# Layer 1's decode rows: sums over partitions in plain float32, four rows at a time in the four column groups

## The chip, the core and the metric

The kernel runs on one core of one Trainium2 chip. Its engines work side by side, each on its own queue of instructions: TensorE (PE, with its weight loads PEld), VectorE (DVE), ScalarE (ACT), GpSimd (POOL), and SyncE (SP), which here only issues DMAs. The metric is the time of one execution in microseconds on the device, as the median of several runs.

## What is computed

One inference step of two layers, a retention layer and a sliding-window attention layer, for a prompt of 1024 tokens and for eight sample rows of one token each. The change touches the sample rows of the first layer: each row and head has a state S of 256 x 512, which is updated and read with the row's q.

```python
def step(S, inp):
    qc, kc, vc = inp
    inner = jnp.einsum('bthd,bshd->bhts', qc, kc) * dmask[None]
    o = jnp.einsum('bhts,bshe->bthe', inner, vc) \
        + jnp.einsum('bthd,bhde->bthe', qc, S) * cross_decay[None, :, :, None]
    S_new = S * chunk_decay[None, :, None, None] \
        + jnp.einsum('bshd,bshe->bhde', kc * k_decay[None, :, :, None], vc)
    return S_new, o
```

With one token a row this is S_new = g S + k v and o = q S_new, a sum over 256 elements of the head's key dimension. Then o is normed over its 512 values and goes on to the gate and the output projection; S_new is an output.

## The kernel before

**The stage.** The input projection of layer 1 is the first big stage. It is cut into sets of weight columns (q, k and v of each of four heads, then the gates), and each set is computed in seven block products (SEQ7) for each half of the prompt's tokens. All float32 products are made from two fp32r parts, hi and lo, as three matmuls: `product` does this at L333 to L335 for v and at L340 to L342 for the others, into PSUM tiles that the page calls b. `w_hi` (L219, ScalarE) and `w_lo` (L224, VectorE or GpSimd) make the two parts of the weights, `w_sum` (L200 to L209, GpSimd) the sums that the block products need, and `evac` (L369 to L381) takes the results out of PSUM.

**The decode rows.** Beside that stage run the 64 decode rows: four heads (h), two halves of the state's 512 columns (hf), eight rows (b). For one of them `dec_load` fetches the state (st, 128 partitions x 2 x 256) and the row's v; `dec_kv` (L263, ScalarE) and `dec_st` (L266, VectorE) update the state; `dec_y0` (L270, ScalarE) and `dec_y1` (L274, VectorE) multiply it by q and add its two halves, so that yd (128 x 256) is left, to be summed over the 128 partitions. That sum is TensorE's: `dec_yh` (L278, ScalarE) and `dec_yl` (L282, GpSimd) split yd into hi and lo, and `dec_mm` (L288, L289) multiplies both by `oneh_r[:, b, :]`, a stationary 128 x 8 of which column b is ones. So row b of the PSUM tile od (8 x 256 for each hf) collects the sum. There is one buffer for yl, two for yh and yd.

**Behind a head's 16 rows.** `dec_n1` to `dec_n4` norm od (8 x 512), `dec_tr` makes four transposes of it (L103, through `tr`), and `dec_ev` copies the result to odT, which a later stage reads.

**What sets the order.** All engines run in the order in which the code is written, which a small planner makes: the block products fill slots one after the other on a planned clock (`slot`, `prod_slot`), and all other work gets a planned time (`when`). Row by row the planner adds STEP = 5.3 us to t0; a row's steps stand at t0 plus 10.5 (kv), 12.3 (st), 13.9 (y0), 15.3 (y1), 16.8 (yh), 18.2 (yl) and 20.4 (the two matmuls), and the end of a head at offsets from its last matmuls (m). Matmuls are held in a list of their own (pes) and are put ahead of the first slot that starts after their time. The planned times set only the order; the engines run as semaphores let them.

**The one-hot.** It comes as 64 columns of the constant c1, is loaded at L645 and cast to fp32r at L653 on VectorE.

Of the kernel before, what the change touches and what calls it, by code (L numbers as in the profile page):

```python
# [7 lines left out]
F32 = mybir.dt.float32  # L8
F32R = mybir.dt.float32r
AF = mybir.ActivationFunctionType  # L10
# [6 lines left out]
ND = 8  # L17
# [17 lines left out]
def make_consts():  # L35
    p = np.arange(128, dtype=np.float64)
    ident = np.eye(128)
    mask = np.zeros((128, H, 128))
    kdec = np.zeros((128, H, NCH))
    epsg = np.zeros((128, H))  # L40
    for h in range(H):
        g = GAM[h]
        mask[:, h, :] = np.where(p[None, :] >= p[:, None], g ** (-(p[:, None] + 1.0)) / 16.0, 0.0)
        for c in range(NCH):
            kdec[:, h, c] = g ** (SREF - 128.0 * c - p - 1.0) / 16.0
        epsg[:, h] = EPS * g ** (-2.0 * (p + 1.0))
    onehot = np.zeros((128, 8, 8))
    for b in range(8):
        onehot[:, b, b] = 1.0
    c1 = np.concatenate([a.reshape(128, -1) for a in (ident, mask, kdec, epsg, onehot)], 1)  # L50
# [12 lines left out]

def trunk(tc, x_prompt, x_sample, state_ret, cache_k, cache_v, norm_ret, w_in_ret, ret_out_norm,
          w_out_ret, norm_swa, w_in_swa, q_norm, k_norm, sinks, w_out_swa, c1, c2,
          y_p, y_s, nrp, nrs, nkp, nvp, nks, nvs):
    nc = tc.nc
    ctx = ExitStack()
    with ctx:
        ctx.enter_context(tc.manual_schedule(engines=MS))  # L70
        _trunk(ctx, tc, nc, locals())


def _trunk(ctx, tc, nc, a):
# [20 lines left out]
    mm = nc.tensor.matmul  # L95
# [6 lines left out]
    def tr(out, in_, ident, start=True, stop=True):  # L102
        nc.tensor.matmul(out, in_, ident, is_transpose=True, start=start, stop=stop)  # L103


    ident = cp.tile([128, 128], F32, name="ident")
# [25 lines left out]
    dcp = sa.enter_context(tc.tile_pool(name="dcp", bufs=1, reuse_waits="tile"))  # L132
# [11 lines left out]
    oneh_r = dcp.tile([128, 8, 8], F32R, name="oneh_r")  # L144
    warm = dcp.tile([1, 8], F32, name="warm")

    XT = {}
# [95 lines left out]
    heads = [dict() for _ in range(H)]  # L243
# [4 lines left out]
    def dt(name, bufs, sh=(128, 256), dt_=F32):  # L248
        return dpo[0].tile(list(sh), dt_, name=name, bufs=bufs)

    def sview(x, h, hf, b):
        return x[0, b, h, :, hf * 256:hf * 256 + 256].rearrange("(f p) e -> p f e", p=128)
# [13 lines left out]
        dve.scalar_tensor_tensor(d["st"], d["st"], GAM[h], d["kv"], MUL, ADD)  # L266

    def dec_y0(d, h, hf, b):
        d["yd"] = dt("yd", 2)
        act(d["yd"], d["st"][:, 0, :], AF.Copy, scale=heads[h]["qd"][:, 0, b:b + 1])  # L270
        nc.sync.dma_start(out=sview(nrs, h, hf, b), in_=d["st"])

    def dec_y1(d, h, hf, b):
        dve.scalar_tensor_tensor(d["yd"], d["st"][:, 1, :], heads[h]["qd"][:, 1, b:b + 1], d["yd"], MUL, ADD)  # L274

    def dec_yh(d, h, hf, b):
        d["yh"] = dt("yh", 2, dt_=F32R)
        act(d["yh"], d["yd"], AF.Copy)  # L278

    def dec_yl(d, h, hf, b):  # L280
        d["yl"] = dt("yl", 1, dt_=F32R)
        pool.tensor_tensor(d["yl"], d["yd"], d["yh"].bitcast(F32), SUB)  # L282

    def dec_mm(d, h, hf, b):
        if hf == 0 and b == 0:
            heads[h]["od"] = odp.tile([128, 512], F32, name="od")
        od = heads[h]["od"][0:8, hf * 256:hf * 256 + 256]
        mm(od, oneh_r[:, b, :], d["yh"], start=(b == 0), stop=False)  # L288
        mm(od, oneh_r[:, b, :], d["yl"], start=False, stop=(b == ND - 1))  # L289

    def dec_n1(h):
        d = heads[h]
        d["on"] = ring("c")[0:8, 0:512]
        d["ss"] = dcp.tile([128, 1], F32, name="oss", bufs=2)
        act(d["on"], d["od"][0:8, :], AF.Square, accum_out=d["ss"][:8])

    def dec_n2(h):
        ss = heads[h]["ss"][:8]
        dve.tensor_scalar(ss, ss, 1.0 / DV, EPS, MUL, ADD)

    def dec_n3(h):
        ss = heads[h]["ss"][:8]
        rsq(ss, ss, 1)

    def dec_n4(h):
        d = heads[h]
        dve.tensor_scalar(d["on"], d["od"][0:8, :], d["ss"][:8], None, MUL)

    def dec_tr(h):
        pt = heads[h]["pt"] = odp.tile([128, 512], F32, name="od")  # L310
        for i in range(4):
            tr(pt[:, i * 8:i * 8 + 8], heads[h]["on"][:, i * 128:i * 128 + 128], ident[:8, :8])

    def dec_ev(h):
        dve.tensor_copy(odT[:, 4 * h:4 * h + 4, :], heads[h]["pt"][:, :32].rearrange("p (i t) -> p i t", i=4))


    SEQ7 = (("A11", B11, 0, True), ("S2", T2, 1, True), ("S1", T1, 2, True), ("A12", B21, 0, False),
# [90 lines left out]

    gb = sp.tile([128, D], F32, name="gb")  # L410
    gl = sp.tile([25, 128], F32, name="gl")
    onehot = sp.tile([128, 64], F32, name="onehot")
# [128 lines left out]
    def later(n, fn, *a):  # L541

        at.setdefault(n, []).append((fn, a))

    def when(t, fn, *a):
        ev.append((t, len(ev), fn, a))
# [106 lines left out]
    later(14, lambda: dve.tensor_copy(oneh_r, onehot.rearrange("p (b m) -> p b m", b=8)))  # L653

    later(17, lambda: [fn(T3, c) for c in (5, 7) for fn in (th, tl)])
    later(18, dsums, 1, (T3,))
# [7 lines left out]
    for s in sets[2:]:  # L664
# [31 lines left out]
        for r in range(2 * s.subs):  # L696
            free = raws[-5] + 1.6
            need = min(reads[r])
            t = max(free, need - 13.0)
            t = raw_t[0] = max(t, raw_t[0] + 0.01)  # L700
# [18 lines left out]
            s.end = clock[0]  # L719

    STEP, GAP = 5.3, 6.5
    pes = []
# [85 lines left out]
    for n, s in enumerate(slots):  # L808
        while pes and pes[0][0] <= s.t:
            _, fn, args = pes.pop(0)  # L810
# [7 lines left out]
        while ev and ev[0][0] < end:  # L818
            _, _, fn, args = ev.pop(0)
# [33 lines left out]
    kdec = M01[:, 256:288].rearrange("p (h c) -> p h c", h=H)  # L853
    epsg = M01[:, 288:292]
# [886 lines left out]
    out = so_all()  # L1741
# [49 lines left out]
    pt = dec_cache(0)  # L1791
# [5 lines left out]
    pt = dec_cache(1)  # L1797
# [53 lines left out]


def c1w():
    return 128 + 512 + 32 + 4 + 64


def c2w():
# [31 lines left out]
```

## Time and profile before

| | us |
|---|---|
| median of 3 runs | 1369.84 |
| lowest, highest | 1367.8, 1372.5 |
| the profiled execution, its own time | 1371.73 |
| its span, from the first to the last instruction | 1369.9 |
| TensorE busy, its mean granted clock | 1318.6, 0.987 |

How the profile is read: each row of a timeline has the start and the length in us, the engine, the line of the kernel, the operation, out<-in by the kernel's names, the shapes, and how many instructions are merged in it. Matmuls are pipelined and their ends are modelled, so two that follow each other overlap in it; what one costs is the distance from its start to the next one's. A row that names stretches has the busy time of each engine in each, then the granted TensorE clock, the DMA engines' share and GB/s. The chain of waits follows back from the last instruction, step by step, what released it.

### The profile page before, as it was taken

Reading aid. Unit: us, or ns where it says so; the run is one execution under the profiler, and the core shown is the slowest. Engines: PE = TensorE matmul, PEld = TensorE weight load, DVE = VectorE, ACT = ScalarE, POOL = GpSimd, SP = SyncE. Lnnn points to the kernel's source line nnn. Section 1 sums busy time; section 2 is a strip of 40 time slices with the busy share of each in tenths; the row PEclk is TensorE's granted clock in tenths of the full one; section 3 lists DMA queues with packets and bytes.
Section 4 is the critical chain, followed back from the end, with each engine's and each line's share of the span. In section 5 each row is a group of like instructions: output and inputs, shape, how many; then the busy total and the mean of one; then the engine's idle time right before and its main releaser. Section 6 shows DMA issues by size and latency. Waiting matters only on the chain.

```text
span 1369.9 us, 26110 instructions
## 1 busy us (share of the span) xinstructions
PE 1318.6 (96%) x9661; PEld 1235.3 (90%) x9661; DVE 708.4 (52%) x1362; ACT 651.4 (48%) x1625; POOL 762.7 (56%) x886
## 2 busy tenths in 40 slices
PE   6999999999999999898979999998999999999998
PEld 6999999999999999686868889997898999998998
DVE  6943665566556553675751112335555555669421
ACT  5532555555556653675740112244465666657311
POOL 6753656655566753697986553544476666555000
PEclk9999999999999999999989999999999999999999
DMA  6314767667667653556545444442111110103523
GB/s 218 103 56 144 219 212 230 174 217 230 198 216 212 216 155 93 185 175 194 169 149 168 123 154 124 133 132 66 47 48 61 44 41 32 55 17 110 164 83 83
DMA packets 192804, 186.68 MB, mean 136 GB/s; under 512 B 12724, under 2 KB 172524, under 8 KB 192660
## 3 DMA queue, kind: packets, MB, share of 16 engines
q1 hardware_dynamic: 155840, 148.87, 35.8%
q10 hardware_dynamic: 36836, 36.14, 8.2%
q8 instruction: 76, 1.25, 0.4%
q14 instruction: 52, 0.43, 0.1%
HBM read 128.59 MB, written 57.41 MB: 136 GB/s over the span
## 4 chain that ended last, share of the span: by engine, by line
PE 87%; DVE 4%; POOL 3%; DMA 2%; issue 2%; ACT 1%; SPq 0%; ACTq 0%; POOLq 0%; DVEq 0%
PE b L340 7%; PE b L342 7%; PE b L341 7%; PE pj L1090 6%; PE pj L1091 6%; PE pj L1092 6%; PE pj L1141 4%; PE pj L1139 4%; PE pj L1140 4%; PE b L334 4%; PE b L333 4%; PE b L335 4%; PE tr L103 4%; PE o L1554 2%; PE tr L862 1%
## 5 line engine op out<-in xcount | busy, mean ns | idle before, releaser
L340 PE MATMUL b<-xh,woh 128*128 128x258 f32 x784 | 222.2, 283 | 0.0
L342 PE MATMUL b<-xh,wol 128*128 128x258 f32 x784 | 221.7, 283 | 0.0
L341 PE MATMUL b<-xl,woh 128*128 128x258 f32 x784 | 221.4, 282 | 0.0
L1090 PE MATMUL pj<-A_hi,wh 128*128 128x384 f32 (+1 forms) x512 | 178.6, 349 | 0.0
L1091 PE MATMUL pj<-A_lo,wh 128*128 128x384 f32 (+1 forms) x512 | 165.2, 323 | 0.0
L1092 PE MATMUL pj<-A_hi,wl 128*128 128x384 f32 (+1 forms) x512 | 165.1, 323 | 0.0
L340 PEld LDWEIGHTS b<-xh,woh 128*128 128x128 f32 x784 | 148.1, 189 | 1.2
L341 PEld LDWEIGHTS b<-xl,woh 128*128 128x128 f32 x784 | 148.7, 190 | 0.0
L342 PEld LDWEIGHTS b<-xh,wol 128*128 128x128 f32 x784 | 148.1, 189 | 0.0
L1080 POOL TENSOR_TENSOR wl<-wr,wh 128x1024 fp32r<-128x1024 f32 (+1 forms) x60 | 115.1, 1929 | 43.4 <-DVE wh L1079 20.1
L334 PE MATMUL b<-wol,xh 128*128 128x256 f32 x448 | 126.0, 281 | 1.2 <-DVE wol L224 1.2
L333 PE MATMUL b<-woh,xh 128*128 128x256 f32 x448 | 125.8, 281 | 0.0
L335 PE MATMUL b<-woh,xl 128*128 128x256 f32 x448 | 125.7, 281 | 0.0
L1090 PEld LDWEIGHTS pj<-A_hi,wh 128*128 128x128 f32 x512 | 97.3, 190 | 10.3 <-issue 9.6
L282 POOL TENSOR_TENSOR yl<-yd,yh 128x256 fp32r<-128x256 f32 x64 | 56.4, 881 | 80.9 <-PE od L289 39.0
L1091 PEld LDWEIGHTS pj<-A_lo,wh 128*128 128x128 f32 x512 | 97.5, 190 | 0.0
L1092 PEld LDWEIGHTS pj<-A_hi,wl 128*128 128x128 f32 x512 | 97.1, 190 | 0.0
L1531 POOL TENSOR_TENSOR s<-s,sm 128x512 f32<-128x512 f32 x64 | 68.0, 1062 | 50.2 <-DVE sm L1530 48.3
L224 POOL TENSOR_TENSOR wol<-raw,woh 128x512 fp32r<-128x512 f32 x52 | 68.9, 1332 | 48.1 <-ACT woh L219 47.3
L334 PEld LDWEIGHTS b<-wol,xh 128*128 128x128 f32 x448 | 84.3, 188 | 1.4 <-DVE wol L224 1.4
L333 PEld LDWEIGHTS b<-woh,xh 128*128 128x128 f32 x448 | 84.3, 188 | 0.7
L335 PEld LDWEIGHTS b<-woh,xl 128*128 128x128 f32 x448 | 84.4, 188 | 0.0
(360 smaller groups left out, 3704.9 us busy)
## 6 DMA issues: line engine op xcount, KB each, us to landing
raw<-in_w_in_ret_dram ACTq DMA_DIRECT2D x44, 512.0 KB
st<-in_state_ret_dram SPq DMA_DIRECT2D x64, 256.0 KB
out_dram<-st SPq DMA_DIRECT2D x64, 256.0 KB
wr<-in_w_out_ret_dram SPq DMA_DIRECT2D x32, 512.0 KB
wr<-in_w_in_swa_dram SPq DMA_DIRECT2D x18, 512.0 KB
vb<-vscr SPq DMA_DIRECT2D x64, 128.0 KB
evp<-qks SPq DMA_DIRECT2D x32, 256.0 KB
evx<-vsc SPq DMA_DIRECT2D x32, 256.0 KB
```

What stands on the lines that cost most here:

```text
L224: eng.tensor_tensor(lo, src_of(s, name, sub), hi.bitcast(F32), SUB)
L333: mm(dst, xh, wh, start=a and i == 0, stop=False, skip_group_check=True)
L334: mm(dst, xh, wl, start=False, stop=False, skip_group_check=True)
L335: mm(dst, xl, wh, start=False, stop=z, skip_group_check=True)
L340: mm(dst, wh, xh, start=a, stop=False, **sg)
L341: mm(dst, wh, xl, start=False, stop=False, **sg)
L342: mm(dst, wl, xh, start=False, stop=z, **sg)
L1080: lo_eng[0].tensor_tensor(lo[:, js, :], raw[:, i:i + step, :], hi.bitcast(F32)[:, js, :], ALU.subtract)
L1090: mm(ps, hi[:, k, fs], xh[:, k, t0:t1], start=first and k == ks[0], stop=False)
L1091: mm(ps, hi[:, k, fs], xl[:, k, t0:t1], start=False, stop=False)
L1092: mm(ps, lo[:, k, fs], xh[:, k, t0:t1], start=False, stop=last and k == ks[-1])
L1531: nc.gpsimd.tensor_tensor(st[:, :, 0:256], st[:, :, 0:256], sm.unsqueeze(2).broadcast_to([128, 2, 256]), ALU.mult)
```

## The change

The split into yh and yl goes, and with it `dec_yh`, `dec_yl` and their two steps in the plan. The matmuls of four rows (b = 4r to 4r + 3) are issued together, 18.0 us behind the fourth row's t0, and in plain float32: row g of the four goes to partitions 32 g to 32 g + 31 of od, with a stationary of 128 x 32 (`oneh[:, r, :]`) of which column r is ones. So a group of rows is four matmuls, each in its own 32 columns of the array; r is 0 or 1, and of the 128 partitions of od eight hold a row (0, 1, 32, 33, ...) and the others zeros. The norm then works on 128 partitions, the transposes are 128 x 128, and `dec_ev` picks out the eight. The one-hot is filled by GpSimd at the start in place of the load and the cast; yd has five buffers.

```diff
     def dec_y0(d, h, hf, b):
-        d["yd"] = dt("yd", 2)
+        d["yd"] = dt("yd", 5)
...
-    def dec_yh(d, h, hf, b):
-        d["yh"] = dt("yh", 2, dt_=F32R)
-        act(d["yh"], d["yd"], AF.Copy)
-
-    def dec_yl(d, h, hf, b):
-        d["yl"] = dt("yl", 1, dt_=F32R)
-        pool.tensor_tensor(d["yl"], d["yd"], d["yh"].bitcast(F32), SUB)
-
-    def dec_mm(d, h, hf, b):
-        if hf == 0 and b == 0:
+    def dec_mm(ds, h, hf, r):
+        if hf == 0 and r == 0:
             heads[h]["od"] = odp.tile([128, 512], F32, name="od")
-        od = heads[h]["od"][0:8, hf * 256:hf * 256 + 256]
-        mm(od, oneh_r[:, b, :], d["yh"], start=(b == 0), stop=False)
-        mm(od, oneh_r[:, b, :], d["yl"], start=False, stop=(b == ND - 1))
+        for g, d in enumerate(ds):
+            mm(heads[h]["od"][32 * g:32 * g + 32, hf * 256:hf * 256 + 256], oneh[:, r, :], d["yd"], start=(r == 0 and hf == 0),
+               stop=(r == 1), skip_group_check=(hf == 1))
...
-            tr(pt[:, i * 8:i * 8 + 8], heads[h]["on"][:, i * 128:i * 128 + 128], ident[:8, :8])
+            tr(pt[:, i * 128:i * 128 + 128], heads[h]["on"][:, i * 128:i * 128 + 128], ident)
...
-        dve.tensor_copy(odT[:, 4 * h:4 * h + 4, :], heads[h]["pt"][:, :32].rearrange("p (i t) -> p i t", i=4))
+        dve.tensor_copy(odT[:, 4 * h:4 * h + 4, :].rearrange("p i (r g) -> p i g r", g=4),
+                        heads[h]["pt"].rearrange("p (i g x) -> p i g x", i=4, g=4)[:, :, :, 0:2])
...
-        nc.scalar.dma_start(out=onehot, in_=a["c1"][:, c1w() - 64:])
...
-    later(14, lambda: dve.tensor_copy(oneh_r, onehot.rearrange("p (b m) -> p b m", b=8)))
...
-                for dt_, fn in ((0.0, dec_load), (10.5, dec_kv), (12.3, dec_st), (13.9, dec_y0), (15.3, dec_y1),
-                                (16.8, dec_yh), (18.2, dec_yl)):
+                for dt_, fn in ((0.0, dec_load), (10.5, dec_kv), (12.3, dec_st), (13.9, dec_y0), (15.3, dec_y1)):
                     when(t0 + dt_, fn, d, h, hf, b)
-                pes.append((t0 + 20.4, dec_mm, (d, h, hf, b)))
-                m = t0 + 20.4
+                ds.append(d)
+                if b % 4 == 3:
+                    pes.append((t0 + 18.0, dec_mm, (ds, h, hf, b // 4)))
+                    ds = []
+                m = t0 + 18.0
...
     dve.memset(warm, 0.0)
+    pool.memset(oneh, 0.0)
+    for r in range(2):
+        pool.memset(oneh[:, r, r:r + 1], 1.0)
```

In dec_n1 to dec_n4 the slices [0:8] and [:8] are gone; that is all that changes there.

TensorE at the fourth row of head 0, before (od is the rows' PSUM tile, b_2138 the next block product's; lines 333 to 335 are the three matmuls of a product):

```order
L354 MATMUL vd<-wol,xdecr 40x256
L288 MATMUL od<-yh,oneh_r 8x256
L289 MATMUL od<-yl,oneh_r 8x256
L333 MATMUL b_2138<-woh,xh 128x256
L334 MATMUL b_2138<-wol,xh 128x256
L335 MATMUL b_2138<-woh,xl 128x256
```

And after, where the product's lines are 323 to 325:

```order
L323 MATMUL b_2021<-woh,xh 128x256
L324 MATMUL b_2021<-wol,xh 128x256
L325 MATMUL b_2021<-woh,xl 128x256
L277 MATMUL od<-yd,oneh 32x256 x4
L323 MATMUL b_2060<-woh,xh 128x256
L324 MATMUL b_2060<-wol,xh 128x256
L325 MATMUL b_2060<-woh,xl 128x256
```

The pair of each row is gone from its place, and the four of a group stand together between two products, a little ahead of where the fourth row's pair stood.

GpSimd in the same part of the program, before (s are sums of weights, wol their lo parts, kd the decayed k of the rows):

```order
L407 TENSOR_SCALAR kd<-evp 128x2
L282 TENSOR_TENSOR yl<-yd,yh 128x256 x2
L224 TENSOR_TENSOR wol<-raw,woh 128x512 x2
L206 TENSOR_TENSOR s_2295<-raw 128x512
L206 TENSOR_TENSOR s_2300<-raw 128x512
L282 TENSOR_TENSOR yl<-yd,yh 128x256
L209 TENSOR_TENSOR s_1966<-raw,s_1966 128x512
L282 TENSOR_TENSOR yl<-yd,yh 128x256
```

And after:

```order
L397 TENSOR_SCALAR kd<-evp 128x2 x2
L221 TENSOR_TENSOR wol<-raw,woh 128x512 x2
L203 TENSOR_TENSOR s_2263<-raw 128x512
L203 TENSOR_TENSOR s_2266<-raw 128x512
L206 TENSOR_TENSOR s_1953<-raw,s_1953 128x512
```

The weights' operations follow each other as before, without the yl between them.

VectorE ahead of the first block products, before (xl are lo parts of the activations):

```order
L498 TENSOR_TENSOR xl<-rT,xh 128x4x2
L653 CAST oneh_r<-onehot 128x64
L224 TENSOR_TENSOR wol<-raw,woh 128x512 x2
L224 TENSOR_TENSOR wol<-s_904,woh 128x512
L224 TENSOR_TENSOR wol<-s_946,woh 128x512
```

And after:

```order
L487 TENSOR_TENSOR xl<-rT,xh 128x4x2
L221 TENSOR_TENSOR wol<-raw,woh 128x512 x2
L221 TENSOR_TENSOR wol<-s_904,woh 128x512
L221 TENSOR_TENSOR wol<-s_946,woh 128x512
L476 TENSOR_TENSOR xl<-u,xh 128x4x128 x2
```

The cast is gone from ahead of the lo parts; nothing else moved there.

More of the change, by code (lines that the diff above doesn't have):

```diff
@@ L46, in make_consts @@
         epsg[:, h] = EPS * g ** (-2.0 * (p + 1.0))
[L47 to L50, printed above, removed]
+    c1 = np.concatenate([a.reshape(128, -1) for a in (ident, mask, kdec, epsg)], 1)
     u = np.arange(256, dtype=np.float64)
@@ L143, in _trunk @@
     xdecd = dcp.tile([128, 4, 40], F32R, name="xdecd")
-    oneh_r = dcp.tile([128, 8, 8], F32R, name="oneh_r")
+    oneh = dcp.tile([128, 2, 32], F32, name="oneh")
     warm = dcp.tile([1, 8], F32, name="warm")
@@ L274, in dec_y1 @@
         dve.scalar_tensor_tensor(d["yd"], d["st"][:, 1, :], heads[h]["qd"][:, 1, b:b + 1], d["yd"], MUL, ADD)
-    def dec_yh(d, h, hf, b):
-        d["yh"] = dt("yh", 2, dt_=F32R)
-        act(d["yh"], d["yd"], AF.Copy)
-    def dec_yl(d, h, hf, b):
-        d["yl"] = dt("yl", 1, dt_=F32R)
-        pool.tensor_tensor(d["yl"], d["yd"], d["yh"].bitcast(F32), SUB)
-    def dec_mm(d, h, hf, b):
-        if hf == 0 and b == 0:
+    def dec_mm(ds, h, hf, r):
+        if hf == 0 and r == 0:
             heads[h]["od"] = odp.tile([128, 512], F32, name="od")
-        od = heads[h]["od"][0:8, hf * 256:hf * 256 + 256]
-        mm(od, oneh_r[:, b, :], d["yh"], start=(b == 0), stop=False)
-        mm(od, oneh_r[:, b, :], d["yl"], start=False, stop=(b == ND - 1))
+        for g, d in enumerate(ds):
+            mm(heads[h]["od"][32 * g:32 * g + 32, hf * 256:hf * 256 + 256], oneh[:, r, :], d["yd"], start=(r == 0 and hf == 0),
+               stop=(r == 1), skip_group_check=(hf == 1))
     def dec_n1(h):
         d = heads[h]
-        d["on"] = ring("c")[0:8, 0:512]
+        d["on"] = ring("c")[:, 0:512]
         d["ss"] = dcp.tile([128, 1], F32, name="oss", bufs=2)
-        act(d["on"], d["od"][0:8, :], AF.Square, accum_out=d["ss"][:8])
+        act(d["on"], d["od"], AF.Square, accum_out=d["ss"])
     def dec_n2(h):
-        ss = heads[h]["ss"][:8]
+        ss = heads[h]["ss"]
         dve.tensor_scalar(ss, ss, 1.0 / DV, EPS, MUL, ADD)
     def dec_n3(h):
-        ss = heads[h]["ss"][:8]
+        ss = heads[h]["ss"]
         rsq(ss, ss, 1)
@@ L306, in dec_n4 @@
         d = heads[h]
-        dve.tensor_scalar(d["on"], d["od"][0:8, :], d["ss"][:8], None, MUL)
+        dve.tensor_scalar(d["on"], d["od"], d["ss"], None, MUL)
     def dec_tr(h):
@@ L411, in _trunk @@
     gl = sp.tile([25, 128], F32, name="gl")
-    onehot = sp.tile([128, 64], F32, name="onehot")
     rdec = sp.tile([128, 8, ND], F32, name="rdec")
@@ L721, in _trunk @@
     STEP, GAP = 5.3, 6.5
-    pes = []
+    pes, ds = [], []
     t0 = 0.0
@@ L1853, in c1w @@
 def c1w():
-    return 128 + 512 + 32 + 4 + 64
+    return 128 + 512 + 32 + 4
 def c2w():
```

## The prediction

> **What bounds the kernel now.** I read the busy table of the page first, then the busy time by stretches, then the chain of waits inside the stretch that the change touches.
>
> ```profile
> PE 1318.6 (96%) x9661; PEld 1235.3 (90%) x9661; DVE 708.4 (52%) x1362; ACT 651.4 (48%) x1625; POOL 762.7 (56%) x886
> ```
>
> TensorE is busy 96% of the span and no other engine over 56%. The decode rows' matmuls lie between 135 and 512 us, so I asked for that stretch alone, and for the chain that ends last in it.
>
> ```profile
> core 0: us, PE busy (x) PEld busy (x) DVE busy (x) ACT busy (x) POOL busy (x), PEclk, DMA share, GB/s
> 135.00:512.00 377.00, 377.00 (x3158) 372.37 (x3157) 224.12 (x373) 210.01 (x481) 230.19 (x264) 1.00 0.68 208
> by line: PE b L340 20.5%; PE b L342 20.3%; PE b L341 20.3%; PE b L334 10.6%; PE b L333 10.6%; PE b L335 10.5%; PE od L289 2.0%; PE od L288 2.0%; PE vd L353 1.5%; PE vd L354 1.5%; PE od L103 0.4%
> ```
>
> The first row says that TensorE has work in all 377 us, at full clock. The second is stricter: every share of the chain belongs to a PE line, and together they make 100% up to rounding. No wait for VectorE, ScalarE, GpSimd or a DMA ends last anywhere here. So in this stage a microsecond of TensorE's own work is a microsecond of the run, and a microsecond taken from ScalarE or GpSimd is worth nothing. The lines to watch are L288, L289 and L103 of od: 2.0 + 2.0 + 0.4% of 377 us, some 16.6 us.
>
> **The change, part by part.** First what goes from TensorE: two fp32r matmuls for each of 64 rows.
>
> ```profile
> 146.10 0.28 PE L342 MATMUL b<-xh,wol 128*128 128x258 f32 x1
> 146.22 0.28 PE L288 MATMUL od<-yh,oneh_r 128*8 128x256 f32 x1
> 146.33 0.28 PE L289 MATMUL od<-yl,oneh_r 128*8 128x256 f32 x1
> 146.45 0.28 PE L340 MATMUL b<-xh,woh 128*128 128x258 f32 x1
> ```
>
> The durations overlap, so a matmul's price is the distance between starts: 146.10 to 146.45 is three matmuls in 0.35 us, 0.117 each. Removed: 128 x 0.117 = **15.0 us** (the chain's 4.0% of 377 us is 15.1).
>
> What comes: 16 groups of four plain float32 matmuls of 256 columns, each in its own 32 columns of the array. The trace has none with four groups, but it has plain float32 in two column groups, L1554 in the second layer (stationary 64 wide, output in partitions 0 to 63 and 64 to 127). A plain float32 call leaves two matmul records: L862 makes 64 such calls in the program and has 128 records.
>
> ```profile
> L862 PE MATMUL tr<-evp x128: 275/275/553, 547.1 to 697.3; 128*128 128x128 f32 x128
> 983.46 0.34 PE L1090 MATMUL pj<-A_hi,wh 128*128 128x384 f32 x1
> 983.64 0.33 PE L1091 MATMUL pj<-A_lo,wh 128*128 128x384 f32 x1
> 983.81 0.33 PE L1092 MATMUL pj<-A_hi,wl 128*128 128x384 f32 x1
> 984.07 0.44 PE L1554 MATMUL o<-ptf,vv 128*64 128x128 f32 x4
> 984.44 0.44 PE L1090 MATMUL pj<-A_hi,wh 128*128 128x384 f32 x1
> 984.72 0.34 PE L1091 MATMUL pj<-A_lo,wh 128*128 128x384 f32 x1
> ...
> 988.44 0.34 PE L1092 MATMUL pj<-A_hi,wl 128*128 128x384 f32 x1
> 988.71 0.66 PE L1554 MATMUL o<-ptf,vv 128*64 128x128 f32 x8
> 989.29 0.44 PE L1090 MATMUL pj<-A_hi,wh 128*128 128x384 f32 x1
> 989.57 0.34 PE L1091 MATMUL pj<-A_lo,wh 128*128 128x384 f32 x1
> ```
>
> A 384-column neighbour costs 0.175 us (983.46 to 983.81 is two). From the start of the neighbour before to the second start behind is 0.91 us for two calls (x4) and 1.13 for four (x8); less two neighbours, 0.56 and 0.78. So two further calls, one in each column group, cost 0.22: two steps of 0.11, each carrying both groups. What is left, 0.56 - 0.22 = **0.34 us, is fixed**: the price of going into the column groups and out again.
>
> For the new group I take the fixed 0.34 and two steps that carry all four column groups. A step at 256 columns is 2 x 0.11 = 0.22. So 0.34 + 0.44 = 0.78 us a group, 16 x 0.78 = **12.5 us**; TensorE gains 2.5. The unknown is the number of steps a group, since four column groups at once are not in the trace: two if all go together as L1554's two do, four if only pairs do, eight if none (16 x 2.10 = 33.6 us). I take two, the row that is nearest. For the fixed part the other end is nothing, as for L288, whose eight columns cost only 0.117; but L288 is fp32r and never leaves partition 0, and L1554 shares with the new form both type and placing, so I take 0.34.
>
> The four transposes of a head now read 128 rows, not 8.
>
> ```profile
> 233.81 0.28 PE L342 MATMUL b<-xh,wol 128*128 128x258 f32 x1
> 234.03 0.41 PE L103 MATMUL od<-ident,evc 8*128 8x8 f32 x4
> 234.37 0.39 PE L340 MATMUL b<-xh,woh 128*128 128x258 f32 x1
> 234.59 0.29 PE L341 MATMUL b<-xl,woh 128*128 128x258 f32 x1
> 1003.76 0.35 PE L1092 MATMUL pj<-A_hi,wl 128*128 128x384 f32 x1
> 1003.94 0.60 PE L103 MATMUL tr<-ident,s 128*128 128x128 f32 x4
> 1004.30 0.42 PE L1090 MATMUL pj<-A_hi,wh 128*128 128x384 f32 x1
> 1004.55 0.33 PE L1091 MATMUL pj<-A_lo,wh 128*128 128x384 f32 x1
> ```
>
> By the same reckoning the small ones cost 0.78 - 2 x 0.12 = 0.54 us and full ones 0.79 - 2 x 0.175 = 0.44: a transpose 16 times as large is cheaper, because it does not leave the full array. Four heads: **-0.4 us**.
>
> The cast of the one-hot goes, and it stood on VectorE right before an operand that TensorE waited for.
>
> ```profile
> 70.45 0.18 DVE L653 CAST oneh_r<-onehot 128x64 fp32r<-128x64 f32 x1
> 70.55 2.37 DVE L224 TENSOR_TENSOR wol<-raw,woh 128x512 fp32r<-128x512 f32 x2
> 72.37 0.39 PE L334 MATMUL b<-wol,xh 128*128 128x256 f32 x1 [1.19 <-DVE wol L224]
> ```
>
> TensorE idles 1.19 us until that product; the cast pushes it back 0.10 (70.45 to 70.55), at most its 0.18. I take **-0.1 us**.
>
> What costs or brings nothing:
>
> ```profile
> L282 POOL TENSOR_TENSOR yl<-yd,yh 128x256 fp32r<-128x256 f32 x64 | 56.4, 881 | 80.9 <-PE od L289 39.0 <-ACT yh L278 28.0 <-ACT yd L270 6.6
> L278 ACT ACTIVATE yh<-yd 128x256 fp32r<-128x256 f32 x64 | 26.3, 411 | 36.9 <-DVE yd L274 34.6 <-PE od L289 1.3 <-PE b L342 0.9
> 403.66 1.18 DVE L274 SCALAR_TENSOR_TENSOR yd<-st,qd,yd 128x256 f32<-128x256 f32 x1 [2.31 <-ACT yd L270]
> 407.22 0.28 PE L340 MATMUL b<-xh,woh 128*128 128x258 f32 x1
> 4.30 0.18 POOL L437 TENSOR_SCALAR ss<-ss 8x1 f32<-8x1 f32 x1 [3.05 <-ACT junk L433]
> ```
>
> - yh and yl: 26.3 us of ScalarE, 56.4 of GpSimd and 80.9 us of GpSimd's waits go, most of these for TensorE itself. They lie beside a TensorE that never waits, so the gain is 0.
> - The new wait: a group is issued when the last of its four yd is due. The tightest of the 16 is the last group of head 2: the order puts it just ahead of the product whose first matmul starts at 407.22 before the change, and its last yd ends at 403.66 + 1.18 = 404.84. That leaves 2.4 us, and no other group has less. Were it late, all products queued behind it on TensorE would wait, microsecond for microsecond.
> - Five yd buffers: a buffer comes round after five rows, when its group has been issued at least one row's step (5.3 us by the planner) earlier.
> - The norm over 128 partitions in place of 8, and the copy of the same 32 values: off TensorE, and the four transposes are still issued 7.6 us by the planner behind the last group.
> - Three small fills on GpSimd at the start lie in its 3.05 us of idleness; the one-hot's load is gone. SP's order is the same as before, row for row.
>
> The sum: -2.5 - 0.4 - 0.1 = **-3.0 us**. The profiled execution took 1371.73 us with a span of 1369.9, so 1.8 lie around it; it should become 1368.7 and its span 1366.9. The median of the runs shown, 1369.84, is 1.9 below the profiled one; from it I get **1366.8 us**, 0.2% less.
>
> **Rivals.** *The column groups go in order.* Each call's second half needs the columns of its first. If TensorE took the records strictly as they stand, a call's first half could only go with the second half of the call before: four calls would take five steps, not two. For L1554 this would read one, two, one; the trace has two, then two:
>
> ```profile
> L1554 PE MATMUL o<-ptf,vv x2: 323/323/323, 984.1 to 984.1; 128*64 128x128 f32 x2
> L1554 PE MATMUL o<-ptf,vv x4: 273/298/323, 984.1 to 984.2; 128*64 128x128 f32 x4
> ```
>
> These are the records up to 984.10 and up to 984.30: two start together, and two more together behind them. That speaks for one queue a column group, and against this rival; with four groups the look ahead is longer, and that is not shown. Its time: x4 would be three steps, so the fixed part 0.56 - 0.33 = 0.23; a group 0.23 + 5 x 0.22 = 1.33, 16 of them 21.3, hence +6.3 - 0.5 = +5.8 us, **1375.6**. The point: a group replaces 8 x 0.117 = 0.94 us, so with 0.34 fixed the third step of 0.22 (1.00) already loses. The Trainium skill, "TensorE: Matmul & The Clock Gate", in "Part 3: Packing small matmuls — row/col tiling", holds that matmuls start and end strictly in program order; by that rule this rival is what happens, and the paired starts above disagree with it.
>
> *Pairs or singles only.* Four steps: 16 x 1.22 = 19.5, so +4.5 - 0.5 = +4.0, 1373.8; eight: +18.1, 1387.9. For it: nothing shows four at once. Against: L1554's second group costs nothing.
>
> *The seam behind the stage.*
>
> ```profile
> 551.50:555.60 4.10, 0.00 (x0) 0.00 (x0) 1.57 (x3) 2.74 (x7) 1.68 (x2) 0.75 1.04 383
> 555.70:560.40 4.70, 4.70 (x14) 4.02 (x15) 2.29 (x6) 2.41 (x5) 3.01 (x4) 0.50 0.80 278
> ```
>
> At the next stage's start TensorE stands idle for 4.1 us while the DMA engines are full, and then runs 4.70 us at clock 0.50, which loses half of them, 2.35. The change brings all this some 3 us forward. If the low stretch goes with that, 1364.4; if another such appears, 1369.2. The Trainium skill, same page, "Part 1: The HAM clock gate", says that the gate watches a free-running window; so it could fall either way, and no row here shows which.
>
> *The change doesn't do what it says:* excluded, the order has the 16 groups and neither yh nor yl.
>
> **How the numbers follow.** All four together in two steps, seam alike: 0.70. In order: 0.08. Pairs 0.04, singles 0.04. Seam better 0.07, seam worse 0.07. The likeliest gives 1366.8. The range: a seam better by one low stretch, and 1 us for runs that differ, give 1363.4; above, a worse seam or a third step (+3.5, 1370.3), and again most of 1 us, give 1371.0. Left out are in order, pairs and singles, 0.16; the ends of the fixed cost stay out too (none at all would be 16 x 0.34 = 5.4 lower). A measurement tells about 0.3%, 4.1 us, from no change: faster means under 1365.7. That holds for the better seam (0.07) and a sixth of the likeliest (0.12), 0.19; slower for in order, singles and half of pairs, 0.14; the rest, 0.67, is within 0.3%.
>
> **What would show it.** Right: od's new line has records that start four together and four more 0.22 us behind, a group costs 0.78 us between its neighbours, the stage's chain is still all PE, the full transposes cost 0.44. Wrong: starts that come one by one or in pairs, a wait of TensorE for yd, a stage that grows shorter by more than 3 us, or a span that changes behind 546 us only.

## The result, and the profile after

| | before | after |
|---|---|---|
| median, us (22 runs each) | 1369.86 | 1366.21 |
| lowest to highest | 1367.2 to 1375.0 | 1363.7 to 1370.3 |
| ratio of the runs, 95% interval | | 0.9972 (0.9963 to 0.9981) |
| profiled execution, its own time | 1371.73 | 1366.37 |
| its span, mean granted clock | 1369.9, 0.987 | 1364.6, 0.990 |

The forecast was 1366.8 us; 1366.21 came. The medians differ by 0.27%, within the 0.3% named there. The spans differ by 5.3 us, more than the medians, and the end of this section shows why.

The changed kernel's page (busy table), then the stretch from 135 to 512 us, then the chain of waits in it:

```profile
PE 1313.3 (96%) x9661; PEld 1225.7 (90%) x9661; DVE 699.7 (51%) x1361; ACT 629.5 (46%) x1561; POOL 708.1 (52%) x825
```

```profile
135.00:512.00 377.00, 377.00 (x3182) 367.73 (x3182) 217.06 (x376) 188.30 (x417) 175.11 (x200) 1.00 0.68 208
```

```profile
by line: PE b L330 21.1%; PE b L332 20.6%; PE b L331 20.5%; PE b L323 10.9%; PE b L324 10.6%; PE b L325 10.5%; PE od L277 2.4%; PE vd L344 1.5%; PE vd L343 1.5%; PE od L100 0.5%
```

GpSimd lost 55 us of work in this stretch (230.19 to 175.11) and ScalarE 22, but TensorE is still busy in all 377.00, and the chain is still PE alone, so none of the 55 counts. What counts stands in od: L288 and L289 with 4.0% have become L277 with 2.4%.

TensorE's timeline of the changed kernel at one group, and then at the four transposes of a head:

```profile
222.17 0.28 PE L332 MATMUL b<-xh,wol 128*128 128x258 f32 x1
222.38 0.64 PE L277 MATMUL od<-yd,oneh 128*32 128x256 f32 x8
222.95 0.39 PE L330 MATMUL b<-xh,woh 128*128 128x258 f32 x1
223.17 0.28 PE L331 MATMUL b<-xl,woh 128*128 128x258 f32 x1
...
230.16 0.28 PE L332 MATMUL b<-xh,wol 128*128 128x258 f32 x1
230.28 0.60 PE L100 MATMUL od<-ident,evc 128*128 128x128 f32 x4
230.63 0.36 PE L330 MATMUL b<-xh,woh 128*128 128x258 f32 x1
230.84 0.28 PE L331 MATMUL b<-xl,woh 128*128 128x258 f32 x1
```

Four plain float32 calls are eight records (x8). By the prediction's reckoning a group costs 223.17 - 222.17 less two neighbours of 0.12, 0.76 us (0.760 to 0.770 over the groups, from the unrounded starts); the transposes cost 230.84 - 230.16 - 0.24 = 0.44. How the eight start shows in the records of L277 up to 201.45 and up to 201.75, for the group at 201.41:

```profile
L277 PE MATMUL od<-yd,oneh x4: 403/403/403, 201.4 to 201.4; 128*32 128x256 f32 x4
L277 PE MATMUL od<-yd,oneh x8: 379/391/403, 201.4 to 201.7; 128*32 128x256 f32 x8
```

Four start within 0.02 us, and four more 0.24 us behind: two steps.

To see what the stage gained, I take the same matmuls of the block products in both traces (beside od's there are 9517 matmul records in each, in the same order) and compare their starts. Here is one early in the stretch and the stage's last one, before and then after:

```profile
136.95 0.29 PE L341 MATMUL b<-xl,woh 128*128 128x258 f32 x1
546.23 0.28 PE L342 MATMUL b<-xh,wol 128*128 128x258 f32 x1
```

```profile
136.88 0.29 PE L331 MATMUL b<-xl,woh 128*128 128x258 f32 x1
543.18 0.28 PE L332 MATMUL b<-xh,wol 128*128 128x258 f32 x1
```

The stage is shorter by 409.28 - 406.30 = **2.98 us** (2.99 from the unrounded starts, which I use from here on). At 136.9 us the changed kernel is only 0.07 ahead, since in this execution its first matmul started 0.44 later. Between the product matmuls at 63.8 and at 89.3 us it had made up **0.53** (from the unrounded starts); here are these two, before and then after:

```profile
63.79 0.88 PE L556 MATMUL b<-xl,woh 128*128 128x258 f32 x6
89.28 0.28 PE L333 MATMUL b<-woh,xh 128*128 128x256 f32 x1
64.27 0.51 PE L545 MATMUL b<-xl,woh 128*128 128x258 f32 x3
89.21 0.28 PE L323 MATMUL b<-woh,xh 128*128 128x256 f32 x1
```

That is the place of the cast; here are VectorE, GpSimd and TensorE there, after:

```profile
71.28 2.38 DVE L221 TENSOR_TENSOR wol<-raw,woh 128x512 fp32r<-128x512 f32 x2
73.58 0.68 DVE L221 TENSOR_TENSOR wol<-s,woh 128x512 fp32r<-128x512 f32 x1
71.30 1.81 POOL L197 TENSOR_TENSOR s<-raw 128x512 f32<-128x512 f32 x1
72.02 0.39 PE L324 MATMUL b<-wol,xh 128*128 128x256 f32 x1 [0.36 <-DVE wol L221]
```

TensorE waits 0.36 us for wol where it waited 1.19.

**Behind the stage** the two profiled executions part by another 2.4 us: the stage's last product matmul starts 3.05 us earlier than before (546.23 against 543.18), the last matmul of all 5.44. There is no changed work there, but there are stretches at half clock. The sums over those of each kernel behind 546 us, before (six) and after (four), each row with TensorE's busy time in them:

```profile
sum 33.00, PE 27.27 PEld 22.64 DVE 12.09 ACT 12.91 POOL 21.17; mean PE 4.54 PEld 3.77 DVE 2.02 ACT 2.15 POOL 3.53
```

```profile
sum 26.70, PE 20.35 PEld 17.14 DVE 9.71 ACT 9.05 POOL 13.40; mean PE 5.09 PEld 4.29 DVE 2.43 ACT 2.26 POOL 3.35
```

TensorE works 6.9 us less at clock 0.50 in the execution after, which is up to 3.5 us. That is the execution, not the change. In a second profile of the changed kernel (the last experiment) the clock at this place is back at 1.00 from 555.9 us on, where here it is 0.50 until 558.8; and the 22 runs of the changed kernel have spans of 1361.9 to 1362.1 where their mean clock is 0.991 and of 1366.5 to 1368.5 at 0.986. Runs of equal clock show the change better. In the spans that the runs list, the mean after is 1362.0 at 0.991, 1363.3 at 0.990 and 1364.4 at 0.989; 21 runs of the kernel before, beside the first experiments, have 1365.3, 1366.0 and 1367.1. That is 2.7 to 3.3 us at equal clock, from runs that were not taken side by side.

### The profile page after: what moved, and what is told of

It is laid out like the page before. It is cut to its first block, busy times and chain, and to the rows that moved or that the text cites. A ratio compares the mean times of both kernels' runs of the same rounds, so it can differ in the third digit from the quotient of the medians.

```text
span 1364.6 us, 25935 instructions
## 1 busy us (share of the span) xinstructions
PE 1313.3 (96%) x9661; PEld 1225.7 (90%) x9661; DVE 699.7 (51%) x1361; ACT 629.5 (46%) x1561; POOL 708.1 (52%) x825
## 4 chain that ended last, share of the span: by engine, by line
PE 85%; DVE 5%; DMA 3%; POOL 3%; issue 2%; ACT 1%; SPq 0%; ACTq 0%; POOLq 0%; DVEq 0%
PE b L330 7%; PE b L332 7%; PE b L331 7%; PE pj L1082 6%; PE pj L1084 6%; PE pj L1083 6%; PE pj L1133 5%; PE pj L1131 4%; PE pj L1132 4%; PE b L323 4%; PE b L324 4%; PE b L325 4%; PE tr L100 4%; PE o L1546 2%; PE sc L1508 1%
## 5 line engine op out<-in xcount | busy, mean ns | idle before, releaser
L1515 ACT ACTIVATE s<-s,mx 128x257 f32<-128x257 f32 x128 | 64.0, 502 | 31.6 <-DVE mx L1513 27.9
```

## The experiments

The theory: a group is a fixed price plus two steps that carry four column groups each; the cast delayed TensorE; all else is worth nothing. Against it: the starts of column groups could have another cause than the columns, the relief of GpSimd or ScalarE could be what pays, and the 0.53 us could be the lost load or an accident. Where a time of the stage is given, it is the start of the stage's last product matmul less that of the one at 136.9 us, against before's.

**Only two column groups at a time.** Each group of rows uses two column groups, each of them twice, in the same number of calls (`dec_ev` picks the rows out accordingly):

```diff
-        for g, d in enumerate(ds):
-            mm(heads[h]["od"][32 * g:32 * g + 32, hf * 256:hf * 256 + 256], oneh[:, r, :], d["yd"], start=(r == 0 and hf == 0),
-               stop=(r == 1), skip_group_check=(hf == 1))
+        for q in (0, 2, 1, 3):
+            g, x = 2 * r + q // 2, q % 2
+            mm(heads[h]["od"][32 * g:32 * g + 32, hf * 256:hf * 256 + 256], oneh[:, x, :], ds[q]["yd"], start=(x == 0 and hf == 0),
+               stop=(x == 1), skip_group_check=(hf == 1))
```

> The four rows of a group go to two column groups, two rows in each (rows 0 and 1 of the tile's quarter), in place of four; the outputs are the same. Theory (column groups run side by side, one column group takes its own matmuls one after the other): four steps of 0.22 us in place of two, so a group costs about 0.33 + 4 x 0.22 = 1.20 us between its neighbours in place of 0.765, starts come in pairs, and the stage ends 16 x 0.44 = 7.0 us later than with the change, about 4 us later than before it. Rival (a plain float32 group is bound by something other than the columns, such as the loads of the stationary or a fixed drain): the group stays near 0.77 us and the stage's end does not move.

It took 1373.02 us. TensorE at a group:

```profile
222.95 0.28 PE L333 MATMUL b<-xh,wol 128*128 128x258 f32 x1
223.16 1.06 PE L278 MATMUL od<-yd,oneh 128*32 128x256 f32 x8
224.15 0.39 PE L331 MATMUL b<-xh,woh 128*128 128x258 f32 x1
224.37 0.28 PE L332 MATMUL b<-xl,woh 128*128 128x258 f32 x1
```

The same eight records now cost 224.37 - 222.95 - 0.24 = 1.18 us (1.18 to 1.19 over the groups), and start in four pairs 0.22 to 0.24 us apart. The stage is 3.6 us longer than before, 6.6 longer than with the change. So the rounds are set by the column groups, one record of each at a time: with pairs the change would have lost.

**Eight rows in one burst**, so that the fixed price is paid 8 times and not 16. It needs eight yd, for whose room st and vb give up a buffer each:

```diff
-        d["st"] = dt("st", 4, (128, 2, 256))
+        d["st"] = dt("st", 3, (128, 2, 256))
...
-        d["vb"] = dt("vb", 3)
+        d["vb"] = dt("vb", 2)
...
-        d["yd"] = dt("yd", 5)
+        d["yd"] = dt("yd", 8)
...
-        for g, d in enumerate(ds):
-            mm(heads[h]["od"][32 * g:32 * g + 32, hf * 256:hf * 256 + 256], oneh[:, r, :], d["yd"], start=(r == 0 and hf == 0),
-               stop=(r == 1), skip_group_check=(hf == 1))
+        for r in range(2):
+            for g in range(4):
+                mm(heads[h]["od"][32 * g:32 * g + 32, hf * 256:hf * 256 + 256], oneh[:, r, :], ds[4 * r + g]["yd"],
+                   start=(r == 0 and hf == 0), stop=(r == 1), skip_group_check=(hf == 1))
...
-                if b % 4 == 3:
-                    pes.append((t0 + 18.0, dec_mm, (ds, h, hf, b // 4)))
+                if b == 7:
+                    pes.append((t0 + 18.0, dec_mm, (ds, h, hf, 0)))
```

> Eight rows in one burst of eight matmuls, first the four column groups with r = 0, then the four with r = 1: 8 bursts in place of 16. For room, yd has 8 buffers, st 3 and vb 2. Theory (a fixed price of about 0.33 us for going into the column groups and out, plus 0.22 us a step): a burst costs 0.33 + 4 x 0.22 = 1.21 us, 8 of them 9.7 in place of 16 x 0.765 = 12.2, so the stage ends 2.5 us earlier than with the change and the time is about 1363.7, 6 us under before. Rival 1 (the price is by the matmul, not by the burst): 1.53 us a burst, no gain. Rival 2 (fewer buffers make the rows late, and TensorE waits for yd): bursts stand behind a wait and the gain is lost or turned.

The median was 1376.88, a ratio of 1.0053 (1.0037 to 1.0070): slower, though seven of the eight bursts cost 1.19 to 1.20 us and the kernel was 4.8 us ahead of before at 361 us. It then lost 9. TensorE at two places of that loss, and five rows of its list of waits between 380 and 515 us (who waits for whom: us, times, the longest; SPq is SyncE's queue of DMAs, and L253 loads a state):

```profile
403.98 1.06 PE L278 MATMUL od<-yd,oneh 128*32 128x256 f32 x14
406.29 0.62 PE L278 MATMUL od<-yd,oneh 128*32 128x256 f32 x2 [1.25 <-DVE yd L271]
...
492.06 0.39 PE L331 MATMUL b<-xh,woh 128*128 128x258 f32 x1 [2.71 <-ACT woh L216]
```

```profile
ACT kv L260 <- DMA vb<-vscr: 23.3, 10, 3.7
DVE st L263 <- ACT kv L260: 16.3, 9, 2.8
DVE wol L221 <- ACT woh L216: 15.6, 4, 6.0
ACT woh L216 <- DMA gsc<-evw: 9.9, 2, 6.1
SPq L253 <- DMA out_dram<-st: 59.2, 17, 6.1
```

The last row is where it begins: with three st buffers SyncE's queue stands at the load of a state until an older state has been stored, 59.2 us in all, where the kernel before has a single such wait of 1.2. Behind that load stand the row's v and the stores of the gates (gsc). So ScalarE was held at kv, for v, and at the weights' split, for a store of the gates, and TensorE waited for the last yd and for woh. The loads of v waited only some 4 us of their own, so the rows put it on st more than on vb; no run changes the one without the other. The burst is right and the buffers were wrong; so the price of eight rows needs a version with room.

**The same, column group by column group**: both calls of a column group right behind each other, so that twelve records stand ahead of the first one of the last column group. To start in the same round as the first of the others it has to pass nine of them.

```diff
-        for r in range(2):
-            for g in range(4):
+        for g in range(4):
+            for r in range(2):
```

> As the burst of eight, but the matmuls stand column group by column group: two for the first, two for the second, and so on, so four matmul records of one column group stand ahead of the next group's first. Theory (each column group has its own queue and TensorE looks far enough ahead): the same 1.21 us a burst, starts in fours. Rival (the look ahead is short, or the order is kept): starts no longer come in fours, up to 13 steps in order, 0.23 + 13 x 0.22 = 3.1 us a burst, 8 x 1.9 = 15 us more than the burst of eight.

It took 1369.98 us. A burst, and the records of L278 up to 220.95:

```profile
220.67 0.28 PE L333 MATMUL b<-xh,wol 128*128 128x258 f32 x1
220.88 1.09 PE L278 MATMUL od<-yd,oneh 128*32 128x256 f32 x16
221.90 0.39 PE L331 MATMUL b<-xh,woh 128*128 128x258 f32 x1
222.13 0.28 PE L332 MATMUL b<-xl,woh 128*128 128x258 f32 x1
```

```profile
L278 PE MATMUL od<-yd,oneh x4: 403/403/404, 220.9 to 220.9; 128*32 128x256 f32 x4
```

Four still start together, 13 to 14 ns apart where it was 7, and the burst costs 222.13 - 220.67 - 0.24 = 1.22 us (1.21 to 1.22 from the unrounded starts) in place of 1.20. A record does not name its column group in the trace; that the four are one of each follows from the pairs above. So TensorE takes the records of one column group one after the other, and the first record of the last one starts ahead of nine that stand before it. The distances fit a simple picture, which no run tests further: between two first records stand one more record in the first order and three more in this one, so 7 and 13 to 14 ns are about 3.4 ns a record (an estimate from these starts), as if the records were handed out in program order and each column group then kept its own waiting. Of the two waits that the kernel with the first burst had, this one had only that near 490 us.

**The kernel before without the cast** and its load; GpSimd fills the one-hot at the start:

```diff
-    onehot = sp.tile([128, 64], F32, name="onehot")
...
-        nc.scalar.dma_start(out=onehot, in_=a["c1"][:, c1w() - 64:])
...
-    later(14, lambda: dve.tensor_copy(oneh_r, onehot.rearrange("p (b m) -> p b m", b=8)))
...
+    pool.memset(oneh_r.bitcast(F32), 0.0)
+    for b in range(8):
+        pool.memset(oneh_r.bitcast(F32)[:, b, b:b + 1], 1.0)
```

> The kernel before, with the one-hot of 128 x 8 x 8 filled by GpSimd at the start in place of its load and its cast on VectorE; nothing else is changed. The traces of before and after differ by 0.53 us around the cast at 70 us, where 0.1 (at most 0.18) was forecast, and by 0.44 us the other way at the first matmul. Theory A (the cast is worth about 0.5 us, since VectorE has to wait for the load or be started anew): between 64 and 89 us TensorE gains 0.4 to 0.6 us on before. Theory B (0.1, and the rest is of that one execution): a gain of 0.1 to 0.2. If GpSimd's fills at the start are what moved the first matmul by 0.44, it is late here too, since there are nine of them in place of three; if not, it stands at 7.1 us give or take what differs from run to run.

The median was 1367.27, a ratio of 0.9983 (0.9971 to 0.9995). In the trace the first matmul starts 0.02 later than before's, in spite of nine fills; between 63.8 and 89.3 us the kernel gains 0.87, more than either theory gave, and of the wait for wol 0.2 us are left, at the weight load; from 136.9 us on it stays 0.94 ahead to the end of the stage. So the cast, or its load, was worth several times the 0.1 forecast.

**Eight rows with room.** The first burst version, but the product k v is no longer kept: ScalarE scales st in place, VectorE adds v times k. The state and the outputs are the same sums. That frees kv, so st and vb keep four and three buffers; the one-hot is 33 columns wide, read at an offset.

```diff
     def dec_kv(d, h, hf, b):
-        d["kv"] = dt("kv", 1, (128, 2, 256))
-        for f in range(2):
-            act(d["kv"][:, f, :], d["vb"], AF.Copy, scale=heads[h]["kd"][:, f, b:b + 1])
+        act(d["st"], d["st"], AF.Copy, scale=GAM[h])
 
     def dec_st(d, h, hf, b):
-        dve.scalar_tensor_tensor(d["st"], d["st"], GAM[h], d["kv"], MUL, ADD)
+        for f in range(2):
+            dve.scalar_tensor_tensor(d["st"][:, f, :], d["vb"], heads[h]["kd"][:, f, b:b + 1], d["st"][:, f, :], MUL, ADD)
...
```

> The burst of eight once more, but with st and vb at four and three buffers as in the changed kernel. The room for eight yd comes from kv: ScalarE multiplies the state by its decay in place, and VectorE adds v times k in two instructions of 256 columns in place of one of 512. Theory (the first burst of eight lost only by its fewer buffers: v and states came late, and TensorE waited; its bursts themselves cost the 1.20 us that was expected): no wait at the bursts, 8 x 1.20 = 9.6 us in place of 16 x 0.765 = 12.2, the stage's end 2.6 us ahead of the changed kernel's, and a time of about 1363.6. Rival (ScalarE, held at the ninth row's yd until a burst has read the first, is late with the weights' hi parts each time): TensorE waits for woh behind the bursts, 0.5 us or more each, and the time is that of the changed kernel or longer.

The median was 1363.31 where before had 1369.01 on the same chip: 0.9960 (0.9947 to 0.9974). One burst:

```profile
220.06 0.28 PE L332 MATMUL b<-xh,wol 128*128 128x258 f32 x1
220.27 1.07 PE L277 MATMUL od<-yd,oneh 128*32 128x256 f32 x16
221.28 0.39 PE L330 MATMUL b<-xh,woh 128*128 128x258 f32 x1
221.50 0.29 PE L331 MATMUL b<-xl,woh 128*128 128x258 f32 x1
```

It costs 221.50 - 220.06 - 0.24 = 1.20 us (1.19 to 1.20 from the unrounded starts). The stage is 5.94 us shorter than before, 3.0 more than with the change. With 0.765 for two steps and 1.195 for four, a step is 0.215 us and the **fixed price 0.335**, if all steps cost alike: the two terms of the prediction, 0.22 and 0.34. What the fixed part is made of, no run shows.

**That edit alone**, four rows a group as in the change:

> The changed kernel with the update of the state as in the roomy burst of eight (no kv) and nothing else. Theory: ScalarE and VectorE have room, TensorE does not wait, the stage's end stays within 0.3 us of the changed kernel's; so what the roomy burst of eight gains or loses is the burst's. Rival: two VectorE instructions for one make VectorE late somewhere, and the stage's end moves by a microsecond or more.

1367.31 us in a single run; the stage is 2.99 us shorter than before, as with the change. The edit of kv is worth nothing, so the 3.0 us are the burst's. At the bursts themselves 16 x 0.765 - 8 x 1.195 = 2.7 are to be seen; the other 0.3 is spread over the products, none of which moved by more than 0.02, and stays open.

**The relief put back**: the change, with a copy of yd on ScalarE and one on GpSimd for each row, in the places of yh and yl; the groups are issued 20.4 us behind t0, as the pairs were:

```diff
+    def dec_yh(d, h, hf, b):
+        act(d["yd"], d["yd"], AF.Copy)
+
+    def dec_yl(d, h, hf, b):
+        pool.tensor_tensor(d["yd"], d["yd"], onec[:, 0:1].broadcast_to([128, 256]), MUL)
```

> The changed kernel with as much work put back on ScalarE and GpSimd as the split was: yd is copied onto itself on ScalarE, then multiplied by ones on GpSimd, in the places of yh and yl, and the groups are issued 20.4 us behind t0 as the pairs were. The outputs are the same. Theory (TensorE's own work alone sets this stage): ScalarE and GpSimd get their 64 instructions each back, and the stage's end stays where the changed kernel has it, within 0.3 us. Rival (the relief of ScalarE and GpSimd is part of the gain): the stage ends 0.5 to 2 us later.

1365.21 us in a single run, and the stretch reads:

```profile
135.00:512.00 377.00, 377.00 (x3182) 367.77 (x3181) 222.88 (x376) 209.95 (x481) 217.03 (x264) 1.00 0.68 208
```

ScalarE is back at 210 us and GpSimd at 217 of its 230, and the stage is still 2.91 us shorter than before. The relief is worth nothing that can be seen.

**The cast put back**: the change, with a cast of 64 columns, used by nothing, where the one-hot's cast was:

```diff
+    dum = sp.tile([128, 64], F32R, name="dum")
...
+    later(14, lambda: dve.tensor_copy(dum, ident[:, 0:64]))
```

> The changed kernel with a cast of 128 x 64 put back on VectorE, ahead of the first lo parts of the weights, where the one-hot's cast was; nothing reads it. Theory (VectorE and GpSimd take turns: the 0.18 us of the cast let GpSimd's sum of 1.3 us go ahead of the lo part that TensorE waits for): TensorE idles about 1.2 us at 72 us in place of 0.4 or less, and loses 0.5 to 0.9 us between 64 and 89 us. Rival (the load of the one-hot or something else of the start made the difference): it idles no longer than in the changed kernel, and loses at most the 0.2 us of the cast.

1363.73 us in a single run at a clock of 0.991, so the trace has to decide. VectorE, GpSimd and TensorE:

```profile
70.43 0.18 DVE L643 CAST dum<-ident 128x64 fp32r<-128x64 f32 x1
70.53 2.36 DVE L221 TENSOR_TENSOR wol<-raw,woh 128x512 fp32r<-128x512 f32 x2
70.44 1.29 POOL L197 TENSOR_TENSOR s<-raw 128x512 f32<-128x512 f32 x1
72.34 0.39 PE L324 MATMUL b<-wol,xh 128*128 128x256 f32 x1 [1.52 <-DVE wol L221]
```

TensorE waits 1.52 us, and between 63.8 and 89.3 us the kernel is 0.32 slower than before where the change was 0.53 faster: 0.85 us for a cast that nothing reads. No load came back with it, so it is the cast and not the load. The stage behind is 2.99 shorter, as with the change.

**The change and the roomy burst once more**, on one chip, to compare them with each other:

> The changed kernel as it is, beside the roomy burst of eight on one chip. The first matmul stood 0.44 us later in its first profile than before the change. If that was of that one execution, it stands at 7.0 to 7.3 us here, and the time is 1366 to 1367, some 3.5 us under before; if the change moved the start, it stands at 7.5 us again.

> The roomy burst of eight, unchanged. By the stage's end (2.9 us ahead of the changed kernel's, counted from the first burst's product on) its time should be 2 to 4 us under that of the changed kernel in the same call. Rival: its first result owed something to the chip or to the clock, and the two are within a microsecond.

The change: median 1366.77, 0.9982 (0.9972 to 0.9991). The burst: 1364.68 in five runs, 0.9960 (0.9948 to 0.9973), so 2.1 us less. Their stages are 2.99 and 5.94 us shorter than before, as in their first profiles. The change's first matmul starts at 7.05 us here, 7.08 before, and the burst's at 7.54 where it was 6.97 in its first profile: so the 0.44 belonged to the one execution and not to the change. By the medians the change is 2.6 us under before and not the 3.5 expected; at equal clock (0.991, 0.989, 0.988) its spans are 3.7, 3.3 and 3.2 us shorter than before's on this chip. The burst beats both kernels by its trace; by the times the two intervals against before just overlap.

## Why the prediction came out right

| term, us | forecast | measured |
|---|---|---|
| 16 x (group in - four pairs out) | -2.5 (0.78, 0.94) | -2.5 (0.765, 0.92) |
| transposes, 4 heads | -0.4 | -0.4 |
| the stage, 136.9 us to its end | -2.9 | -2.99 |
| the cast | -0.1 | -0.53 in the profile after |
| relief of ScalarE and GpSimd, new wait, fills | 0 | 0 |

(A pair's price before is its neighbours' distance less 0.12, 0.231 us on average over the 64; the forecast took 0.234.)

- **The bound.** The stage is TensorE's work alone, before and after: its chain is all PE, and 77 us less on the two other engines moved nothing; putting the work back moved nothing either.
- **Four column groups in two steps.** The step that was taken from L1554 with two column groups held with four: starts in fours, 0.76 us a group. The pairs show the price of the rival, 1.18 us a group, near the 1.22 reckoned for it.
- **In order: fallen.** TensorE took four first halves and then four second halves, which strict order would not allow, and column group by column group a record started ahead of nine that stand before it in the program. The Trainium skill, "TensorE: Matmul & The Clock Gate", in "Part 3: Packing small matmuls — row/col tiling", has matmuls start in program order; these starts of plain float32 calls in different column groups disagree with it.
- **The fixed price.** Two burst sizes give 0.335 us, beside L1554's 0.34, so the end "nothing" of its range is out.
- **The transposes.** 0.44 us, as reckoned from the full ones of the second layer.
- **The new wait.** TensorE does not wait for yd in the stage. It did in the first version with eight rows, and every product queued behind it was late, as the prediction had it. Of the 80.9 us of GpSimd's waits, 39.0 were for TensorE, so not most of them; they were worth nothing either way.
- **The cast: sized too small.** The step that was off is "the cast pushes it back 0.10, at most its 0.18". It was read on VectorE alone. One of the signs of being wrong is met by it: from 63.8 us on, with the place of the cast, the stage is 2.99 + 0.53 = 3.52 us shorter, which is more than 3. With GpSimd's row beside it the place looks different; before:

```profile
70.46 1.31 POOL L200 TENSOR_TENSOR s<-raw 128x512 f32<-128x512 f32 x1
```

The cast held VectorE until wol could start at 70.55, and GpSimd's sum had started at 70.46. So the sum ran first, in 1.31 us, and wol, which takes 0.68 when alone, reached TensorE 1.8 us after its start. Without the cast wol starts at 71.28, GpSimd at 71.30, and now GpSimd's sum is the stretched one, 1.81, while wol is there after 0.74. As the rows read, the two work one at a time, and 0.02 to 0.09 us decide whose turn is first. Taking the cast away from the kernel before and putting it back into the change move this wait as that reading says; the turns themselves are read from the rows. The Trainium skill, "GPSIMD Engine Reference", in "1. Specifications", says that GpSimd shares its way into the memory with VectorE, and that VectorE's instructions of two inputs contend there; these rows agree. With the cast away two outcomes appear, 0.53 to 0.57 us gained in most profiles and 0.87 to 0.90 in three; in the first wol starts 0.3 us later, counted from TensorE's matmuls ahead of it. What sets it is open. The kernel before is of the second sort by that count, and the change with the cast put back of the first, so like for like the cast would cost 0.87 and 0.85, and the 0.53 would be that less the 0.3.
- **The seam.** No row told which way the stretches at half clock would fall, and the runs say that they fall differently from run to run of one kernel. As a rival of this change it was none; it is the spread of both kernels. In this pair of profiles the stretch at the seam was equally long, 6.8 us in each.

The total, -3.0 forecast, is -3.5 by stage and cast, -2.7 to -3.7 by spans of equal clock, and -3.65 by the medians (-2.6 on the chip of the last experiment). The half microsecond of the cast, which the forecast lacked, is hidden in the runs' spread of 6.5 us. So the stage's -2.9 came by its mechanism, term by term; that the median came within 0.6 us of 1366.8 is in part luck.

## What to carry to other kernels

Sums over partitions with few result rows are cheap in column groups if four go together and the way in and out is paid seldom: price them as a fixed part plus steps, and find both from two burst sizes. Before a burst is made longer at the cost of buffers, ask what waits in the same DMA queue behind a load that needs one of them. And where a small instruction stands just ahead of an operand that TensorE waits for, read VectorE's and GpSimd's rows side by side, since it can cost a whole turn of the other engine.

## What the runs showed of the hardware

- Plain float32 calls in four column groups start 7 ns apart in rounds of four, and 13 to 14 ns apart when they stand column group by column group: there a record starts ahead of nine that come before it in the program.
- Leaving the full array for the column groups and coming back costs some 0.335 us, against 0.215 for a whole step of 256 columns in all four (from bursts of two and of four steps, at 0.765 and 1.195 us).
- VectorE's and GpSimd's elementwise operations on two inputs took turns: 0.68 us became 1.8, and 1.3 became 1.8, by who came 0.02 to 0.09 us earlier.
- Runs of one kernel spread over 6.5 us with mean clocks of 0.986 to 0.991, some 1 us for each 0.001 (mean spans of 1367.2 at 0.986 and 1362.0 at 0.991); the stage itself took 409.28 us in two profiles without the groups of four and 406.30 in four with them (406.38 in the one with the work put back), so a stage tells changes apart that the medians hardly do.
